# Second layer's head: the norm's and gate's four vectors loaded before the experts' summed rows

## The chip, the cores and the metric

The kernel runs on one core of a Trainium2 chip. What is measured is the device time of one execution in microseconds (us), as the median of several runs. The kernel before took 1263.39 us (three runs: 1258.64, 1263.39 and 1264.37).

## What is computed

Two layers of a generator over 256 latent tokens and 256 context tokens of 1024 numbers each. A layer normalizes and modulates its input, puts it through one projection for four kinds of attention, projects back, and ends in a mixture of 16 experts (two for each token). What matters here is the seam between the layers: the first layer's last line, and the second layer's first.

```python
for l in range(DEPTH):
    ...
    h = _layer_norm(x) * (1 + sc1) + sh1
    ...
    x = _layer_norm(ALPHA * x + g2 * _hier_moe(_layer_norm(x) * (1 + sc2) + sh2, *moe_p),
                    ln2_g[l], ln2_b[l])
    if with_ctx:
        ...
        xc = _layer_norm(ALPHA * xc + g2c * _hier_moe(_layer_norm(xc) * (1 + sc2c) + sh2c, *moe_p),
                         ln2_g[l], ln2_b[l])
```

Four vectors of 1024 numbers belong to the first layer's last line: the gate `g2` of the latent tokens, the gate `g2c` of the context tokens, and `ln2_g` and `ln2_b`. Each is spread over 128 partitions by its load, so that each load writes 128 rows of 4096 bytes.

## The kernel before

In the first layer every expert gathers its tokens' rows, runs three products, and scatters its weighted results into `yD`, a buffer in DRAM that has two rows for each token (one for each of its two experts). The very last expert's result does not go through DRAM: it stays on the core as a table `yh`, `yl` with a one-hot matrix `oh` (`combine`, L1804 and L1805), and is added by matmuls.

The second layer starts in `attention` (branch `if not full`, from L448 on). Its steps:

- **Row loads.** For each of the four chunks of 128 tokens `base` loads the two `yD` rows of each token (L1788, two loads of 512 KB for a chunk) and TensorE adds them in PSUM with an identity matrix (L1793). Chunks 0 and 1 (latent tokens) go to two `hh` tiles, chunks 2 and 3 (context) to four `s` tiles.
- **Vectors.** `fetch(vec2, vec2)` loads the four vectors by `bcast_to` (L280): key 0 (the gate of the latent tokens, in DRAM as `modD`) and `ln2_g` into one `hh` tile, `ln2_b` and key 1 (the context's gate) into another.
- **Finish.** `finish` adds the last expert (L1818, two matmuls of `kbc`/`vbc` against `qa` for each half row), multiplies by the gate (L1820), adds the residual (L1821), takes the norm (L260, ScalarE's square L262, L1826, rsqrt L222 to L232, L1831). `stream` then norms again and writes the input of the projection (L522 to L525), which TensorE turns (L507) and VectorE and ScalarE modulate (L274, L276) and split into two parts (L497, L498).
- **Weights.** `dslab` (L467) and the first slabs of the input projection (`load_slab`, L412) follow on the same queue, then small tensors: `wkvb` (L652), gains (L655), `wqb` (L657), `win_sink` (L659, 128 x 4 numbers) and the bias rows (L716). A slab is split into two parts by ScalarE (L434) and VectorE or GpSimd (L435). The attention sinks are negated by VectorE at L660.

All these loads are issued by SyncE (SP) in one queue. From `order.__enter__()` to `order.__exit__()` SP's order is the order of the code (`in_order`, a scheduler's manual mode); an SP instruction that waits for a semaphore holds back all that stand behind it. The loads take one of eight semaphores in turn, so that each load also waits for the load eight places ahead of it. VectorE and ScalarE run the lists `STEPS0` and `STEPS1` in the order of the code too, but instructions that stand outside of these lists, such as L660, are placed among them by the scheduler.

The four `hh` tiles take the places of the first layer's expert weights, one place after the other in the order in which the tiles are first written. The place that comes first was last read by the last expert's gate product (L1529), the second holds the last expert's second half of `moe_w_down` and is read until that expert's last matmul (L1548). The other two were set free earlier.

```python
            bases = [base(ch, ys[ch], sums[ch]) for ch in range(4)]
            for b in bases[:2]:
                next(b)
            fetch(vec2, vec2)
            for b in bases[2:]:
                next(b)
```

Of the kernel before, what the change touches and what calls it, by code (L numbers as in the profile page):

```python
# [91 lines left out]
def kern(tc, I, out):  # L92
# [171 lines left out]
    def in_order(*engines):  # L264

        return tc.manual_schedule(engines=set(engines))
# [81 lines left out]
    def attention(l, xs, background, mod2):  # L348
# [48 lines left out]
        def s4(shape, dt=F32):  # L397
            return P1("s4", shape, dt, bufs=9 if full else 12)
# [40 lines left out]
        def hh(shape, dt=F32R):  # L439
            return P0("hh", shape, dt, bufs=4)  # L440
# [9 lines left out]
        if not full:  # L450
            fetch, base, combine, finish = xs
            ys, b2 = ([hh([128, 2, D], F32) for _ in range(2)] for _ in range(2))
            ys = [[y[:, i] for i in range(2)] for y in ys]
            vec2 = {0: b2[0][:, 0], "ln2_g": b2[0][:, 1], "ln2_b": b2[1][:, 0], 1: b2[1][:, 1]}
            t = [s4([128, D]) for _ in range(12)]
            ys += [t[6:8], t[8:10]]
            rs = t[10:] + [r[:, :D] for r in rs]
            order = in_order(mybir.EngineType.SP)
            order.__enter__()
            sums = [[] for _ in range(4)]  # L460
            bases = [base(ch, ys[ch], sums[ch]) for ch in range(4)]
            for b in bases[:2]:
                next(b)
            fetch(vec2, vec2)
            for b in bases[2:]:
                next(b)
        SY.dma_start(dslab, wi[:, 2048:2208].rearrange("(k p) n -> p k n", p=128))  # L467
        ws.append(load_slab(slabs[0][0], (0,)))
# [1404 lines left out]
    for l in range(L):  # L1873
        mod2 = cp.tile([128, 2, 16], F32, name=f"mod2{l}")
        later = vectors((0, 1), (0, 2), (1, 0)) if l == 0 else vectors((1, 1), (1, 2))
        cur = moe(l, attention(l, cur, later, mod2), mod2)
# [28 lines left out]
```

## Time and profile before

| | us |
|---|---|
| median of three runs | 1263.39 |
| lowest and highest run | 1258.64, 1264.37 |
| the profiled execution, its own time | 1259.04 |
| its span in the trace | 1257.2 |
| TensorE busy in the span | 1104.7 (88%) |
| VectorE busy | 670.7 (53%) |
| ScalarE busy | 464.3 (37%) |
| GpSimd busy | 203.8 (16%) |

Times in the trace count from the span's start. The seam lies between about 665 and 745 us. A busy share is an average over the whole kernel; for a change of a few loads in one place, the place has to be read by itself: who waits there, for what, and which wait ends last. In the waits, `SPq` is SyncE's queue of DMA issues. An issue's row gives when SP handed the transfer over, not when the data landed; the landing shows in the start of the instruction that waited for it.

### The profile page before, as it was taken

The page shows a single profiled execution, that of the slowest core. Times are in us where ns is not written, and L with a number is a line of the kernel's source. Part 1 is how long each engine was busy: PE and PEld are TensorE (multiplying, and loading weights), DVE is VectorE, ACT ScalarE, POOL GpSimd, SP SyncE. Part 2 cuts the span into 40 slices and gives each one's busy share as a digit, 9 for nine tenths or more (in the row PEclk, how much of TensorE's full clock was granted, in tenths as well). Part 3 has the DMA queues.
Part 4 walks back from the last instruction along what each step waited for, and adds up shares of the span by engine and source line. Part 5 has one row for each costly group of instructions (what it writes and reads, how often), then busy time and mean ns, then how long its engine had stood idle before and what let it go on. Part 6 is the DMA issues. An engine that isn't in the chain of part 4 may idle for free. (4 is left out here: it accounts for less than half of the span.)

```text
span 1257.2 us, 16382 instructions
## 1 busy us (share of the span) xinstructions
PE 1104.7 (88%) x5962; PEld 701.2 (56%) x5962; DVE 670.7 (53%) x1619; ACT 464.3 (37%) x860; POOL 203.8 (16%) x222
## 2 busy tenths in 40 slices
PE   5999989899962899999898859998898799999995
PEld 2777644366851666666555347764466556455542
DVE  5377167664698785554453578637865611211113
ACT  2332165654242665444353244325643311111110
POOL 0022021212152143222211033200001200000000
PEclk9999999979975899999999979997999699999997
DMA  9943557600746799999995844534715889999993
GB/s 351 317 128 82 199 182 259 234 9 1 243 159 232 256 325 377 387 376 385 389 384 196 286 121 121 193 121 162 233 51 192 302 311 394 394 393 393 394 394 122
DMA packets 147354, 315.79 MB, mean 251 GB/s; under 512 B 20455, under 2 KB 35565, under 8 KB 142145
## 3 DMA queue, kind: packets, MB, share of 16 engines
q1 hardware_dynamic: 143284, 305.98, 68.2%
q0 software_dynamic: 3728, 8.59, 1.9%
q8 instruction: 49, 0.80, 0.3%
q14 instruction: 41, 0.33, 0.1%
q10 hardware_dynamic: 252, 0.09, 0.0%
HBM read 305.45 MB, written 13.70 MB: 254 GB/s over the span
## 5 line engine op out<-in xcount | busy, mean ns | idle before, releaser
L1439 DVE TENSOR_TENSOR hl<-rb,hl 128x1024 fp32r<-128x1024 f32 x71 | 90.7, 1302 | 58.5 <-ACT hl L1437 58.5
L1694 PE MATMUL mm<-rb,xt 128*64 128x256 f32 x816 | 101.0, 383 | 0.0
L1437 ACT ACTIVATE hl<-rb 128x1024 fp32r<-128x1024 f32 x84 | 85.8, 1054 | 34.1 <-PE mm L1449 34.0
L575 PE MATMUL mm<-s,hh 128*128 128x512 f32 x216 | 88.2, 411 | 0.0
L573 PE MATMUL mm<-s,hh 128*128 128x512 f32 x216 | 88.0, 412 | 0.0
L574 PE MATMUL mm<-s,hh 128*128 128x512 f32 x216 | 87.0, 403 | 0.0
L1694 PEld LDWEIGHTS mm<-rb,xt 128*64 128x64 f32 x816 | 58.5, 137 | 35.5 <-issue 9.0
L834 ACT ACTIVATE e<-mm,nmx 128x512 f32<-128x512 f32 (+1 forms) x96 | 58.4, 616 | 27.9 <-DVE nmx L829 17.2
L1448 PE MATMUL mm<-hl,t 128*128 128x512 f32 x144 | 61.7, 428 | 5.9 <-ACT t L1467 3.9
L1450 PE MATMUL mm<-hl,t 128*128 128x512 f32 x144 | 60.0, 419 | 6.7 <-DVE t L1468 6.7
L1449 PE MATMUL mm<-hl,t 128*128 128x512 f32 x144 | 61.7, 429 | 2.9 <-DVE hl L1439 2.7
L829 DVE TENSOR_REDUCE nmx<-mm 128x1 f32<-128x512 f32 (+1 forms) x80 | 52.5, 683 | 5.5 <-PE mm L823 4.5
L1699 DVE TENSOR_TENSOR ta<-ta,mm 128x256 f32<-128x256 f32 x16 | 6.7, 420 | 85.5 <-ACT ta L1698 85.5
L843 POOL TENSOR_SCALAR e<-e,rc 128x256 f32<-128x256 f32 x32 | 30.2, 954 | 123.1 <-DVE rc L841 111.2
L434 ACT ACTIVATE s<-ra 128x1024 fp32r<-128x1024 f32 x30 | 31.2, 1055 | 49.0 <-PE mm L575 22.4
L875 PE MATMUL tr<-cst,e 128*128 128x128 f32 x256 | 44.9, 307 | 4.0 <-DVE e L843 1.4
L573 PEld LDWEIGHTS mm<-s,hh 128*128 128x128 f32 x216 | 40.9, 190 | 13.5 <-issue 3.1
L575 PEld LDWEIGHTS mm<-s,hh 128*128 128x128 f32 x216 | 40.9, 189 | 13.2 <-issue 3.2
L574 PEld LDWEIGHTS mm<-s,hh 128*128 128x128 f32 x216 | 41.0, 190 | 12.3 <-issue 2.6
L1711 PE MATMUL mx<-rb,at 128*64 128x512 f32 x192 | 47.4, 597 | 0.0
L875 PEld LDWEIGHTS tr<-cst,e 128*128 128x128 f32 x256 | 31.9, 154 | 26.8 <-issue 14.5
L321 PE MATMUL mm<-ra,cT 128*32 128x512 f32 x320 | 43.5, 603 | 3.4 <-DMA ra<-in_w_ada_dram 3.4
(542 smaller groups left out, 2342.3 us busy)
## 6 DMA issues: line engine op xcount, KB each, us to landing
rb<-in_moe_w_up_dram SPq DMA_DIRECT2D x52, 1024.0 KB
rb<-in_moe_w_down_dram SPq DMA_DIRECT2D x50, 1024.0 KB
rb<-in_moe_w_gate_dram SPq DMA_DIRECT2D x49, 1024.0 KB
ra<-in_w_ada_dram SPq DMA_DIRECT2D x40, 1024.0 KB
ra<-in_moe_w_gate_dram SPq DMA_DIRECT2D x14, 1024.0 KB
ra<-in_w_in_dram SPq DMA_DIRECT2D x24, 512.0 KB
ra<-in_moe_w_down_dram SPq DMA_DIRECT2D x11, 1024.0 KB
ra<-in_moe_w_up_dram SPq DMA_DIRECT2D x9, 1024.0 KB
```

The lines of the kernel that those rows point to most:

```text
L573: T.matmul(ps, a, hi[:, k2], start=k == 0, stop=False)
L574: T.matmul(ps, a, lo[:, k2], start=False, stop=False)
L575: T.matmul(ps, b, hi[:, k2], start=False, stop=k == KD - 1)
L829: V.tensor_reduce(nmx[:, :nb], ps, axis=AX, op=ALU.max, negate=True)
L834: S.activation(e[:, b], ps[:, b], AF.Exp, bias=nmx[:, b:b + 1], accum_out=sm[:, b:b + 1])
L875: T.transpose(tp[:, k2, 128 * c:128 * c + 128], probs[hh][c][:, 0, 128 * kt:128 * kt + 128], ident)
L1437: S.activation(hi, w[k2], AF.Copy)
L1439: eng.tensor_tensor(lo, w[k2], hi.bitcast(F32), op=ALU.subtract)
L1448: T.matmul(ps[:C], ah, hs[:, k2], start=first and k2 == 0, stop=False)
L1449: T.matmul(ps[:C], ah, ls[:, k2], start=False, stop=False)
L1450: T.matmul(ps[:C], al, hs[:, k2], start=False, stop=last and k2 == 1)
L1694: T.matmul(ps[64 * t:64 * t + 64, j], X[:, k, gi], wt, start=k == 0, stop=k == KD - 1)
```

## The change

The four vector loads stand ahead of all eight row loads; before, they stood behind the first four of them. Nothing else is written differently, and no instruction is added or removed.

```diff
             order.__enter__()
             sums = [[] for _ in range(4)]
             bases = [base(ch, ys[ch], sums[ch]) for ch in range(4)]
-            for b in bases[:2]:
-                next(b)
             fetch(vec2, vec2)
-            for b in bases[2:]:
+            for b in bases:
                 next(b)
```

The file is two lines shorter, so that lines behind this place count two less in the changed kernel (L1788 becomes L1786, L660 becomes L658).

SP's queue at the seam, kernel before: the row loads of chunks 0 and 1, and the vectors. Names that begin with `DMAHW` are the eight semaphores of the loads, `DMASW` those of GpSimd's scatters, `PE` and `DVE` counts of those engines' work.

```order
L1788 DMA hh_6262<-yD 128x1024 [waits DMASW7_49,DMAHW5_49,DMASW0_49,PE_49]
L1788 DMA hh_6262<-yD 128x1024 [waits DMAHW6_49]
L1788 DMA hh_6263<-yD 128x1024 [waits DMAHW7_49,DMAHW4_49,PE_49]
L1788 DMA hh_6263<-yD 128x1024 [waits DMAHW0_49]
L280 DMA hh_6264<-modD_112 128x1024 [waits DMAHW1_49,DVE_49]
L280 DMA hh_6264<-in_ln_g_dram 128x1024 [waits DMAHW2_49]
L280 DMA hh_6265<-in_ln_b_dram 128x1024 [waits DMAHW3_49,DVE_49]
L280 DMA hh_6265<-modD_112 128x1024
```

The same eight loads in the changed kernel:

```order
L280 DMA hh_6264<-modD_112 128x1024 [waits DMAHW5_49,PE_49]
L280 DMA hh_6264<-in_ln_g_dram 128x1024 [waits DMAHW6_49]
L280 DMA hh_6265<-in_ln_b_dram 128x1024 [waits DMAHW7_49,DMAHW4_49,PE_49]
L280 DMA hh_6265<-modD_112 128x1024 [waits DMAHW0_49]
L1786 DMA hh_6262<-yD 128x1024 [waits DMASW7_49,DMAHW1_49,DMASW0_49,DVE_49]
L1786 DMA hh_6262<-yD 128x1024 [waits DMAHW2_49]
L1786 DMA hh_6263<-yD 128x1024 [waits DMAHW3_49,DVE_49]
L1786 DMA hh_6263<-yD 128x1024
```

The waits on the places of the tiles go with the place in the queue, not with the tile: the third load waits in both kernels for the landing and the last use of the last expert's weights (`DMAHW4`, `PE`; both kernels wait for the same counts). It was chunk 1's first row load, and is `ln2_b` now. The waits on the scatters (`DMASW`) move from the first load to the fifth.

VectorE, kernel before: the end of the second norm of chunks 0 and 1, and what follows it. `sink` is the tile of the attention sinks, `ka` and `vad` take the second parts of the first slab.

```order
L522 TENSOR_SCALAR nb_6412<-fin_1481_6324,rs_ya_6399 128x1 [waits DVE_49]
L525 TENSOR_SCALAR s_1470_6277<-x_159,fin_1481_6324,rs_ya_6399 128x1024
L660 TENSOR_SCALAR sink_6242<-sink_6242 128x4 [waits DMAHW2_49]
L435 TENSOR_TENSOR ka_6237<-ra_6293,qbc_6235 128x1024 [waits DMAHW3_49,Activation_49]
L435 TENSOR_TENSOR vad_6247<-ra_6293,vad_6247 128x1024 [waits DMASW7_49,Activation_49]
L276 TENSOR_SCALAR s_1507_6426<-tr_6430,modT_111 128x256 [waits SP_sequencer_49,Activation_49]
```

VectorE in the changed kernel, 18 instructions earlier: the end of the first norm.

```order
L260 TENSOR_SCALAR fin_1481_6324<-fin_1480_6323 128x1 [waits DVE_49]
L1829 SCALAR_TENSOR_TENSOR x_159,fin_1480_6323<-s_1470_6277,rs_yd_6349,hh_6265 128x1024
L658 TENSOR_SCALAR sink_6242<-sink_6242 128x4 [waits DMAHW2_49]
L260 TENSOR_SCALAR fin_1481_6324<-fin_1480_6323 128x1 [waits DVE_49]
L1818 TENSOR_TENSOR biasm_6244<-mm_6362,hh_6265 128x512 [waits DMAHW0_49,DMASW0_49,PE_49]
L1818 TENSOR_TENSOR biasm_6244<-mm_6365,hh_6265 128x512 [waits PE_49]
L1819 SCALAR_TENSOR_TENSOR biasm_6244,fin_1494_6382<-x_28_156,biasm_6244 128x1024 [waits DVE_49]
```

The scheduler now puts the negation of the sinks, which waits for their load, between the last two instructions of the first norm; before, it stood behind the second norm (L525). The rest of VectorE's list is the same here. Some ten instructions of TensorE, VectorE and ScalarE change places once more near the end of the second layer's attention.

## Rows read from the trace of the kernel before

**Rows 1.** Stretches by engine: busy us (instructions), granted clock, DMA share, GB/s

```profile
core 0: us, PE busy (x) PEld busy (x) DVE busy (x) ACT busy (x) POOL busy (x), PEclk, DMA share, GB/s
678.00:696.00 18.00, 15.07 (x90) 9.06 (x87) 7.63 (x9) 4.51 (x6) 3.36 (x2) 1.00 0.00 0
700.00:712.00 12.00, 9.38 (x27) 3.57 (x25) 4.20 (x8) 1.43 (x2) 0.00 (x0) 1.00 0.95 358
...
724.00:738.00 14.00, 6.35 (x25) 5.51 (x26) 8.93 (x24) 6.43 (x9) 0.00 (x0) 0.55 0.58 152
1100.00:1220.00 120.00, 117.46 (x860) 65.42 (x858) 20.23 (x42) 17.35 (x39) 0.00 (x0) 1.00 1.04 393
```

**Rows 2.** Waits of SP's DMA queue, 640 to 760 us: total, times, longest

```profile
SPq L1788 <- DMA yD<-t,idx: 29.6, 2, 23.1
...
SPq L467 <- DMA hh<-modD: 1.9, 1, 1.9
SPq L1788 <- PE mx L1548: 1.4, 1, 1.4
```

**Rows 3.** Timeline of SP at the seam: start, us, what it issues

```profile
697.85 3.41 SPq L1788 DMA_DIRECT2D hh<-yD  x4
...
700.46 0.80 SPq L1788 DMA_DIRECT2D hh<-yD  x2
...
701.37 0.36 SPq L280 DMA_DIRECT2D hh<-modD  x1
...
708.48 0.38 SPq L467 DMA_DIRECT2D ds<-in_w_in_dram  x1
...
722.28 0.71 SPq L659 DMA_DIRECT2D sink<-in_win_sink_dram  x1
```

**Rows 4.** Timeline of TensorE at the seam: start, us, what [idle before <-releaser]

```profile
676.85 1.95 PE L1529 MATMUL mm<-rb,t 128*64 128x256 f32 x16
...
701.99 0.36 PE L162 MATMUL mx<-rec 1*128 1x480 bf16 x1 [1.57 <-DVE vbc L1805]
702.28 3.70 PE L1793 MATMUL mm<-hh,cst 128*128 128x512 f32 x8
...
706.25 0.41 PE L1818 MATMUL mm<-vbc,qa 64*128 64x512 f32 x2
...
710.55 0.40 PE L1818 MATMUL mm<-vbc,qa 64*128 64x512 f32 x2
```

**Rows 5.** Timeline of VectorE at the seam

```profile
708.48 1.29 DVE L1820 TENSOR_TENSOR s<-mm,hh 128x512 f32<-128x512 f32 x2 [6.54 <-DMA hh<-in_ln_g_dram]
...
713.73 0.15 DVE L260 TENSOR_SCALAR fin<-fin 128x1 f32<-128x1 f32 x1
...
721.33 0.15 DVE L260 TENSOR_SCALAR fin<-fin 128x1 f32<-128x1 f32 x1
...
731.57 0.17 DVE L660 TENSOR_SCALAR sink<-sink 128x4 f32<-128x4 f32 x1 [4.38 <-DMA sink<-in_win_sink_dram]
731.65 1.22 DVE L435 TENSOR_TENSOR ka<-ra,qbc 128x1024 fp32r<-128x1024 f32 x1
```

**Rows 6.** Timeline of ScalarE: the first slab's first split

```profile
727.65 1.04 ACT L434 ACTIVATE qbc<-ra 128x1024 fp32r<-128x1024 f32 x1
```

**Rows 7.** The page's second part: GB/s in 40 equal slices of the span

```profile
GB/s 351 317 128 82 199 182 259 234 9 1 243 159 232 256 325 377 387 376 385 389 384 196 286 121 121 193 121 162 233 51 192 302 311 394 394 393 393 394 394 122
```

**Rows 8.** Timeline, 741 to 749 us: three small VectorE operations, and GpSimd beside them

```profile
741.62 2.28 DVE L230 TENSOR_TENSOR rs_td<-rs_td,rs_hd 128x2 f32<-128x2 f32 x1
743.93 2.27 DVE L232 SCALAR_TENSOR_TENSOR rs_yd<-rs_td,rs_yd 128x2 f32<-128x2 f32 x1
746.24 2.26 DVE L229 TENSOR_TENSOR rs_td<-rs_yd 128x2 f32<-128x2 f32 x1
748.53 0.16 DVE L230 TENSOR_TENSOR rs_td<-rs_td,rs_hd 128x2 f32<-128x2 f32 x1
...
741.48 7.00 POOL L435 TENSOR_TENSOR s<-ra,s 128x1024 fp32r<-128x1024 f32 x3 [45.91 <-ACT s L434]
```

## The prediction

> **What bounds the kernel now.** I read the stretches first, then the waits of SP's queue, then SP, TensorE and VectorE in order of time through the seam. The transfers stand still from 678 to 696 us (share 0.00) while the last large expert is computed, and run nearly full, at 358 GB/s, from 700 to 712 us [rows 1]. SP stands at the first row load, longest wait 23.1 us, until the scatters have landed [rows 2]. It issues two row loads at 697.85, and then stands again, for the last expert's last matmul: 1.4 us put down to L1548 in the waits, the next issue at 700.46 [rows 2, 3]. The vectors go out from 701.37 on [rows 3].
>
> TensorE's identity matmuls begin at 702.28, right behind L162 at 701.99, which had waited for VectorE; so chunk 0's rows were in by then. Chunk 0 is added up by 706.66 (706.25 + 0.41), chunk 1 by 710.95 [rows 4]. VectorE is idle 6.54 us until 708.48 [rows 5]. The row names the transfer of `ln2_g`, but SP's next load, which waits for `modD`, goes out at the same 708.48 [rows 2, 3]; what ended the wait was the gate's vector. So VectorE has 1.82 us (708.48 - 706.66) in which it waits for the vector alone. This is what the change can take away at this place.
>
> The seam has a second wait. VectorE stands 4.38 us at L660 until 731.57 for the attention sinks, a load of 2 KB issued at 722.28 behind everything else in the queue [rows 3, 5]. The first split of the weights (L435), which heads the list that leads to the projection, follows it at 731.65 [rows 5]. Behind the seam no slack shows that could take it up: the last experts keep TensorE busy 117.46 of 120 us [rows 1], so I take what the seam loses or wins as it is to the end.
>
> **The change, part by part.**
>
> *Two of four vectors leave the path.* `modD` and `ln2_g` wait for the place that L1529 reads until 678.80 (676.85 + 1.95) [rows 4]. They go out then, into transfers at rest [rows 1], and cost nothing; without that rest they would cost two transfers. VectorE's wait for the gate's vector goes, at most 1.82 us. What is late next is chunk 0 itself.
>
> *The other two come in front of the rows.* `ln2_b` is now the third load, and waits for L1548 as the third load did before: 700.46. All eight row loads stand behind it. The first one takes the place in the queue that `modD` had, fifth, and goes out at about 701.4 instead of 697.85 [rows 3]. When does it land? The nearest rows: from an empty queue, issue to use was at most 4.43 us (697.85 to 702.28); as fifth of a full queue, 7.11 us (701.37 to 708.48) [rows 3 to 5]. The row load is now third behind 700.46, so it lands between 705.8 and 708.5. I take 707.0, between the two. TensorE then starts 4.7 us later than 702.28, and chunk 1 leaves VectorE (L260, 713.73) at 718.4.
>
> *The sinks' wait moves forward.* The negation now stands in front of the L260 that ran at 721.33 [rows 5]. VectorE gets there at about 726.0 (721.33 + 4.7) and waits for the sinks there. Behind it, all of VectorE's 18 instructions from that L260 to L525 stand still, and with them ScalarE, whose L434 at 727.65 follows L524 in its list [rows 6].
>
> *When do the sinks land?* From 700.46 on the queue carries ten loads of 512 KB ahead of the small ones, where it carried twelve from 697.85: the start is 2.61 us later, and two loads are gone. A load is 0.524 MB; at 358 GB/s [rows 1] it takes 1.46 us, and the sinks come 2.61 - 2 x 1.46 = -0.31 us, that is 0.3 us earlier, at 731.26. Bounds: at the fastest slice, 394 GB/s [rows 7], a load takes 1.33 us and they come at 731.52; by the five transfers up to the landing of `modD`, (708.48 - 697.85) / 5 = 2.13 us [rows 3], at 729.92. I take 358 GB/s, which is of this very stretch. The Trainium skill, "DMA: Bandwidth & Descriptors", section "Specifications", gives 435 GB/s as the fabric's ceiling; by it a load would take an estimated 1.21 us, the sinks would come 0.19 us later, and the sum below would be 0.5 us higher. The trace has no slice that fast.
>
> *The sum.* With the sinks at 731.26, L260 starts 0.08 us later (as L435 did behind L660 [rows 5]), at 731.34, which is 10.01 us later than before. ScalarE's first split ends at 728.69 + 10.01 = 738.70 (727.65 + 1.04 [rows 6]), and L435, which needs it, starts there instead of at 731.65: **7.05 us later**. The 4.7 us by which the rows are late vanish in this wait, and the 1.82 us gained do too; they are not added. By the bounds of the sinks' landing the loss is 5.7 to 7.3 us. The instructions that change places near the end of the attention I cost at nothing: they are the same operations, and TensorE has other work beside them.
>
> On the profiled execution this makes 1259.04 + 7.05 = 1266.1 us. That execution and the lowest run (1258.64) lie near 1259, the other two near 1264, and the median, 1263.39, is one of the upper pair. I count from the mean of the four, 1261.36, which gives **1268.4 us**.
>
> **The rivals.**
>
> *The rows alone.* If the 2 KB of sinks land before VectorE needs them, the sinks cost nothing at all. This decides at 726.0: before that, only the 4.7 us count, ScalarE's split ends at 733.39, and L435 is 1.74 us late, or 0.5 us if the rows land at 705.8: at most 1263.1 us. For it: the sinks are small. Against it: they are issued last, and took 9.3 us from 722.28.
>
> *GpSimd's collisions fall elsewhere: not slower.* Three operations of VectorE take 2.28, 2.27 and 2.26 us beside GpSimd's splits, where an undisturbed one takes 0.16 [rows 8]. If GpSimd's first split starts so much earlier or later against VectorE's list that they no longer meet, 6.81 - 3 x 0.16 = 6.33 us come back of the 7.05, and the time is 1262.1. It decides at a shift of some 2.3 us, one such operation. Against it: both engines wait for the same ScalarE splits, so both should shift together. The Trainium skill, "SBUF — State Buffer", section "SBUF: two separate sides", says that the port pair of VectorE and GpSimd is an exclusive lock, held for a whole instruction; by that rule the three do come back when they no longer meet, and the 2.3 us against GpSimd's 7.00 for three agree.
>
> *TensorE's clock falls.* TensorE now has no work from the last expert's end to 707.0. In the stretch from 724 on, which follows a pause, the granted clock is a mean of 0.55 of 2.4 GHz, so mostly 1.2 GHz, while from 700 to 712 it is 1.00 [rows 1]. If chunks 0 and 1 ran at 1.2 GHz throughout, their 8.67 us (702.28 to 710.95 [rows 4]) would double, VectorE would reach the sinks' wait at 734.7, after their landing, and L435 would be 10.4 us late: 1271.8. Up to 5 us of such loss stay hidden in the wait (726.0 to 731.3). The Trainium skill, "TensorE: Matmul & The Clock Gate", section "Part 1: The HAM clock gate (the "warmup" mystery)", has the idle array fall to 1.2 GHz and return only after sustained work; the row from 724 us agrees, and by that rule part of this loss comes, though hardly all.
>
> *The change does what its order says.* If no load waited for L1548, all four vectors would be out of the way, chunk 1 would still leave TensorE at 710.95, and the sinks, four loads earlier, would end VectorE's wait near 725.7: still about 1.5 us late. The order of SP shows that two loads do wait, so I give this no chance of its own.
>
> **How the numbers follow.** The forecast gets 0.60; its own range, bounds and spread of the runs (2.9 us to either side of their mean) together, is 1264.2 to 1271.6. The rows alone get 0.14, the collisions 0.08, the clock 0.13; 0.05 is left for the reordering at the attention's end winning or losing several us. A measurement of this kernel can tell about 0.5% from no change, 6.3 us: from 1257.1 to 1269.7 is the same. The forecast lies across that border: a little over half of it (0.33) is slower, the rest (0.27) the same. The clock is mostly slower (0.10), the first two rivals are the same (0.22). This gives slower 0.44, same 0.52, faster 0.04. The range, 1262 to 1273, takes in most of the two smaller rivals and the clock's.
>
> **What would show it.** Right: `modD` and `ln2_g` issued near 679 us, `ln2_b` at the last expert's end, the first row load about 0.9 us behind it; TensorE's identity matmuls (L1791 there) starting at 706 to 708.5; VectorE's idle time before L658 about 5 us, ending near 731; L435 near 738.7. Wrong: sinks that land before 727, identity matmuls that start before 704, or later stretches that are shorter than before by several us.

## The result and the profile after

The changed kernel took 1268.59 us (median of 14 runs), the kernel before 1262.34 us beside it. The ratio, estimated from the fast runs alone (one of the 14 ran in a slower state), is 1.0055 with an interval of 1.0038 to 1.0072; the medians by themselves give 1.0050. So it is slower, and the size lies on the border of the half per cent up to which the prediction called a time the same. The profiled execution has a span of 1263.7 us against 1257.2. The work is the same. By the page's first part TensorE's busy time grew by 2.7 us, VectorE's and GpSimd's by 0.4 at most, ScalarE's not at all:

```profile
span 1263.7 us, 16383 instructions
...
PE 1107.4 (88%) x5962; PEld 701.3 (55%) x5962; DVE 670.9 (53%) x1619; ACT 464.3 (37%) x860; POOL 204.2 (16%) x222
```

The queue first, as the timeline of SP at the seam; it answers to [rows 3].

```profile
678.48 0.34 SPq L280 DMA_DIRECT2D hh<-modD  x1
678.87 0.43 SPq L280 DMA_DIRECT2D hh<-in_ln_g_dram  x1
700.14 0.33 SPq L280 DMA_DIRECT2D hh<-in_ln_b_dram  x1
...
701.12 2.22 SPq L1786 DMA_DIRECT2D hh<-yD  x4
...
721.27 0.96 SPq L657 DMA_DIRECT2D sink<-in_win_sink_dram  x1
```

Its longest wait between 640 and 760 us, against [rows 2]:

```profile
SPq L280 <- PE mx L1546: 20.7, 1, 20.7
```

Two vectors go out at 678.5, in the quiet. The third waits 20.7 us for the last expert's last matmul, and the first row load stands behind it until 701.12; before it went out at 697.85. Counted from the start of `vbc`, VectorE's last operation for the last expert (701.19 before, 700.86 now), that is 3.60 us later. TensorE's timeline shows what that costs (against [rows 4]):

```profile
701.67 0.36 PE L162 MATMUL mx<-rec 1*128 1x480 bf16 x1 [1.57 <-DVE vbc L1803]
707.43 5.69 PE L1791 MATMUL mm<-hh,cst 128*128 128x512 f32 x8 [5.41 <-DMA hh<-yD]
...
713.72 3.70 PE L1791 MATMUL mm<-hh,cst 128*128 128x512 f32 x8
```

TensorE stands 5.41 us for the rows. Then chunk 0's eight identity matmuls take 5.69 us, where chunk 1's, and chunk 0's before, take 3.70. The stretches of the changed kernel show why (columns as in [rows 1]): the granted clock begins to fall while TensorE stands, is 0.50 of 2.4 GHz, that is 1.2 GHz, when chunk 0 is added, and comes back to 1.00 only between 710 and 712 us.

```profile
704.00:705.00 1.00, 0.00 (x0) 0.00 (x0) 0.00 (x0) 0.00 (x0) 0.00 (x0) 0.82 1.06 397
...
708.00:710.00 2.00, 2.00 (x3) 0.68 (x2) 0.00 (x0) 0.00 (x0) 0.00 (x0) 0.50 1.00 404
710.00:712.00 2.00, 2.00 (x4) 0.87 (x3) 0.00 (x0) 0.00 (x0) 0.00 (x0) 0.63 1.04 424
712.00:714.00 2.00, 2.00 (x8) 0.77 (x7) 0.18 (x1) 0.00 (x0) 0.00 (x0) 1.00 1.02 414
```

VectorE's timeline, which answers to [rows 5]:

```profile
713.82 1.29 DVE L1818 TENSOR_TENSOR s<-mm,hh 128x512 f32<-128x512 f32 x2 [12.21 <-PE mm L1816]
...
730.17 0.17 DVE L658 TENSOR_SCALAR sink<-sink 128x4 f32<-128x4 f32 x1 [1.88 <-DMA sink<-in_win_sink_dram]
...
737.59 1.23 DVE L435 TENSOR_TENSOR ka<-ra,qbc 128x1024 fp32r<-128x1024 f32 x1 [1.53 <-ACT qbc L434]
```

It no longer waits for the gate's vector but for TensorE, and starts at 713.82 instead of 708.48. It reaches the negation of the sinks at 728.29 (730.17 - 1.88), stands there 1.88 us, and L435 starts at 737.59 instead of 731.65: 5.94 us late. From L435 to the end of the span it is 526.11 us, before 525.55. So the seam holds 5.94 of the 6.5 us by which the span is longer.

### The profile page after: what moved, and what is told of

Its sections match the earlier page's. It is cut to its first block, busy times and chain, and to the rows that moved or that the text cites. A ratio compares the mean times of both kernels' runs of the same rounds, so it can differ in the third digit from the quotient of the medians.

```text
span 1263.7 us, 16383 instructions
## 1 busy us (share of the span) xinstructions
PE 1107.4 (88%) x5962; PEld 701.3 (55%) x5962; DVE 670.9 (53%) x1619; ACT 464.3 (37%) x860; POOL 204.2 (16%) x222
```

## The experiments

Executions reach the seam up to 9 us apart, so single profiles are compared by a distance: from the start of `vbc` to the start of L435. It is 737.59 - 700.86 = 36.73 us in the changed kernel and 731.65 - 701.19 = 30.46 in the kernel before (VectorE's timeline, the changed kernel first):

```profile
700.86 0.75 DVE L1803 SCALAR_TENSOR_TENSOR vbc<-mx,tw,kbc 128x512 fp32r<-128x512 f32 x1 [4.60 <-ACT kbc L1802]
...
701.19 0.75 DVE L1805 SCALAR_TENSOR_TENSOR vbc<-mx,tw,kbc 128x512 fp32r<-128x512 f32 x1 [4.60 <-ACT kbc L1804]
```

The table's distances come from such rows. The two theories: the sinks' wait ends last and hides most of the late rows (the prediction), or the late rows themselves are most of the loss. All runs together (the first identity matmul is counted from `vbc` too; "sinks" says how long VectorE stands before the negation; ratios are to the kernel before):

| run | first identity matmul | chunk 0's eight | sinks | L435 | ratio, interval |
|---|---|---|---|---|---|
| before | 1.09 | 3.70 | 4.38 | 30.46 | |
| after | 6.57 | 5.69 | 1.88 | 36.73 | 1.0055 (1.0038 to 1.0072) |
| 1 after, sinks on GpSimd | 6.49 | 6.34 | none | 35.41 | 1.0042 (1.0021 to 1.0063) |
| 2 before, sinks on GpSimd | 1.09 | 3.70 | none | 27.36 | 0.9982 (0.9960 to 1.0003) |
| 3 before, negation early | 1.09 | 3.70 | 10.07 | 37.59 | 1.0087 (1.0064 to 1.0111) |
| 4 rows not held, sinks on GpSimd | 1.09 | 3.70 | none | 27.38 | 0.9966 (0.9947 to 0.9985) |
| 5 after, 28 matmuls added | 6.90 | 3.70 | 0.75 | 33.98 | 1.0033 (1.0008 to 1.0058) |
| 6 run 1, 28 matmuls added | 6.89 | 3.70 | none | 33.17 | 1.0039 (1.0009 to 1.0069) |
| 7 rows not held | 1.10 | 3.70 | 5.55 | 32.97 | 1.0038 (1.0009 to 1.0068) |
| 8 two vectors ahead, sinks on GpSimd | 2.91 | 5.40 | none | 30.90 | 1.0011 (0.9983 to 1.0039) |
| 9 after, 25 matmuls added | 6.66 | 3.70 | 4.13 | 37.07 | 1.0049 (1.0027 to 1.0071) |
| 10 after, sinks loaded first | 6.62 | 5.73 | none | 34.94 | 1.0027 (1.0004 to 1.0050) |
| 11 rows not held, sinks loaded first | 3.73 | 5.40 | none | 31.71 | 0.9999 (0.9977 to 1.0021) |
| 12 the same, behind two vectors | 1.09 | 3.78 | none | 27.46 | 0.9963 (0.9934 to 0.9993) |

### Runs 1 and 2: the sinks taken from VectorE

```diff
-        V.tensor_scalar(sink[:, 1], sink[:, 0], -1.0, None, op0=ALU.mult)
+        (V if full else G).tensor_scalar(sink[:, 1], sink[:, 0], -1.0, None, op0=ALU.mult)
```

Run 1 is the changed kernel with this edit, run 2 the kernel before. Expected of run 1:

> Changed kernel, with the negation of the second layer's sinks on GpSimd instead of VectorE; all else in the same order. It takes the wait for the sinks out of VectorE's list and leaves the late rows. By the prediction's step (rows 4.7 us late, mostly hidden by the sinks) L435 starts 1.7 us later than in the kernel before, near 733.4, and the time is +1.7 us on the kernel before (ratio 1.001). By the trace of the changed kernel (rows late by 7 us, the sinks only 1.9 us of the loss) L435 starts near 735.7, +4.0 us on the kernel before (1.003). If the sinks did not matter at all, it stays at 737.6, +6 us.

Expected of run 2:

> Kernel before, with the same negation on GpSimd. If the sinks' wait at L660 is on the path in the kernel before too, L435 starts when ScalarE's first split ends, at 728.7 instead of 731.65, and the time is 3.0 us shorter (ratio 0.998). If the wait is hidden there, nothing changes (1.000).

Run 1, by the timeline of TensorE and VectorE:

```profile
708.30 0.75 DVE L1803 SCALAR_TENSOR_TENSOR vbc<-mx,tw,kbc 128x512 fp32r<-128x512 f32 x1 [4.60 <-ACT kbc L1802]
714.79 6.34 PE L1791 MATMUL mm<-hh,cst 128*128 128x512 f32 x8 [5.32 <-DMA hh<-yD]
...
743.71 1.23 DVE L435 TENSOR_TENSOR ka<-ra,qbc 128x1024 fp32r<-128x1024 f32 x1 [1.53 <-ACT qbc L434]
```

It shows 35.41, 4.95 us behind the kernel before; its chunk 0 took 0.65 us longer than in the changed kernel. So the late rows, with the slower clock behind them, cost 4 to 5 us against the kernel before, not the 1.7 us that the prediction gave the rows. Run 2 comes out at 27.36: in the kernel before the sinks' wait cost 3.10 us (30.46 - 27.36), as worked out. The distance shows this; the time of run 2 alone (interval 0.9960 to 1.0003) does not. VectorE waits for ScalarE alone there, as its timeline in run 2 shows:

```profile
707.15 0.75 DVE L1805 SCALAR_TENSOR_TENSOR vbc<-mx,tw,kbc 128x512 fp32r<-128x512 f32 x1 [4.60 <-ACT kbc L1804]
...
734.51 1.23 DVE L435 TENSOR_TENSOR ka<-ra,qbc 128x1024 fp32r<-128x1024 f32 x1 [1.53 <-ACT qbc L434]
```

### Run 3: only the negation moved

The loads keep the order of the kernel before. The small loads are written ahead of the list `STEPS0`, and the negation has a step of its own (91) in it:

```diff
-STEPS0 = (90, -1, 90, -2, 0, 0, 0, 0, -3, 0, 0, -4, 1, 0, 2, 3, 0, 1, 4, 5, 0, 1)
+STEPS0 = (90, -1, 90, -2, 0, 0, 0, 0, -3, 0, 0, 91, -4, 1, 0, 2, 3, 0, 1, 4, 5, 0, 1)
```

> Kernel before, loads in its own order, with only the negation moved to the place in VectorE's list that it has in the changed kernel (one instruction later, behind the L260). If a wait for the sinks there is enough to lose the time, VectorE stands about 10 us there until 731.6, L435 starts near 738.9, and the time is +7.3 us (ratio 1.006), with rows that are not late at all. If the late rows are what costs, L435 stays near 731.7 and the time at 1.000. Some instructions behind the seam change places with this edit; L435 is read first.

VectorE's timeline:

```profile
702.44 0.75 DVE L1812 SCALAR_TENSOR_TENSOR vbc<-mx,tw,kbc 128x512 fp32r<-128x512 f32 x1 [4.60 <-ACT kbc L1811]
...
732.63 0.17 DVE L569 TENSOR_SCALAR sink<-sink 128x4 f32<-128x4 f32 x1 [10.07 <-DMA sink<-in_win_sink_dram]
...
740.03 1.23 DVE L435 TENSOR_TENSOR ka<-ra,qbc 128x1024 fp32r<-128x1024 f32 x1 [1.53 <-ACT qbc L434]
```

A wait of 10.07 us for 2 KB, and L435 7.13 us late, with no row late at all. The place of this one instruction is enough to lose, at L435, what the whole change loses. The time lost (ratio 1.0087) is more than the 7.1 us; in the profile some 3 us more lie behind the seam (528.97 us from L435 to the end), where this edit also changes the order. That part was not followed up, and runs 1 and 9 have as much there (528.49 and 529.23).

### Runs 4 and 7: the rows not held

`ln2_b` and the context's gate go through GpSimd's queue; their tile keeps the place that is free only after the last expert.

```diff
-        SY.dma_start(b, bass.AP(tensor=row_ap.tensor, offset=row_ap.offset, ap=[[0, 128], [1, D]]))
+        (q or SY).dma_start(b, bass.AP(tensor=row_ap.tensor, offset=row_ap.offset, ap=[[0, 128], [1, D]]))
...
-            fetch(vec2, vec2)
+            fetch(vec2, (0, "ln2_g")), fetch(vec2, ("ln2_b", 1), G)
```

Run 4 also has the sinks on GpSimd:

> Changed kernel, but ln2_b and the context's gate go through GpSimd's queue (they keep the place that is free only after the last expert), and the sinks are negated on GpSimd as in the first run. If the third load's wait for the last expert is what makes the rows late, the first row load goes out at 697.9 again, the identity matmuls start near 702.3, L435 near 728.7, and the time is 3 us below the kernel before (0.998), as in the second run. If the rows are late for another reason (the transfers, two queues at once), L435 stays near 735.7 as in the first run, +4 us.

Run 7 leaves them on VectorE:

> Changed kernel with ln2_b and the context's gate through GpSimd's queue, as in the fourth run, but the sinks negated on VectorE; the scheduler puts that behind the two L1818 of chunk 2. The rows are early again; only the wait for the sinks is left. If it ends last, VectorE gets to it about 20.6 us after L162 and stands until the sinks land, at 26 to 28.5, and L435 starts at 32 to 34.5, later than in the kernel before (29.66) by 2.5 to 5 us. If the rows were the whole loss, L435 starts at 26.6 as in the fourth run.

The timeline of run 4, SP, TensorE and VectorE:

```profile
701.90 1.75 SPq L1786 DMA_DIRECT2D hh<-yD  x4
705.25 0.75 DVE L1803 SCALAR_TENSOR_TENSOR vbc<-mx,tw,kbc 128x512 fp32r<-128x512 f32 x1 [4.60 <-ACT kbc L1802]
706.34 3.70 PE L1791 MATMUL mm<-hh,cst 128*128 128x512 f32 x8
...
710.74 1.29 DVE L1818 TENSOR_TENSOR s<-mm,hh 128x512 f32<-128x512 f32 x2 [4.74 <-PE mm L1816]
...
715.04 1.29 DVE L1818 TENSOR_TENSOR s<-mm,hh 128x512 f32<-128x512 f32 x2 [1.55 <-PE mm L1816]
...
732.63 1.23 DVE L435 TENSOR_TENSOR ka<-ra,qbc 128x1024 fp32r<-128x1024 f32 x1 [1.53 <-ACT qbc L434]
```

With the third load out of SP's queue the rows are on time: in run 4 the first identity matmul starts 1.09 us after `vbc`, as before, and at full clock. L435 stands at 27.38, and the ratio to the kernel before is 0.9966, with an interval that leaves out 1. But run 2, with the vectors in their old place, has L435 at 27.36. With the sinks out of the way, the early vectors gain nothing at L435: VectorE begins with chunk 0 earlier (5.49 us after `vbc`, before 7.29) and then stands 1.55 us for the sum of chunk 1.

In run 7 VectorE, whose negation the scheduler places a little differently here, stands for the sinks until 26.93 us after `vbc`:

```profile
727.93 0.17 DVE L658 TENSOR_SCALAR sink<-sink 128x4 f32<-128x4 f32 x1 [5.55 <-DMA sink<-in_win_sink_dram]
```

L435 stands at 32.97. With rows on time the sinks' wait alone puts it 5.59 us behind run 4 and 2.51 us behind the kernel before.

### Runs 5, 6 and 9: TensorE kept busy in the pause

```diff
                 ps = mm([128, 512])
+                for _ in range(28 if ch + t == 0 else 0):
+                    T.matmul(ps, last[2][0:64, 0:128], last[0][0:64, :512], start=True, stop=True)
                 for i in range(2):
```

> Changed kernel, with 28 more matmuls (the last expert's table against its one-hot matrix, overwritten by chunk 0's first identity matmul) while TensorE waits for the rows; all that is added is work that nobody reads. Times count from the start of L162. In the changed kernel chunk 0's eight identity matmuls took 5.69 us and L435 starts at 35.9. If the pause lowers TensorE's clock, they now take about 3.7 us. If the sinks' wait ends last, as the prediction has it, VectorE only stands 2 us longer at the negation (3.9 instead of 1.9) and L435 stays at 35.9; the time is that of the changed kernel, +6 us on the kernel before (1.005). If the late rows and the clock end last, L435 comes 2 us earlier, at 33.9.

> The first run (sinks negated on GpSimd) with the same 28 matmuls. There L435 started 34.6 us after L162, and chunk 0's identity matmuls took 6.34 us. If the clock is 2.6 us of that loss, they take 3.7 us and L435 starts at about 32.0, +2.3 us on the kernel before (29.66). If the pause is not what slows them, both stay (34.6).

L162 itself fell behind the added matmuls in both, so they are read from `vbc` (0.81 us ahead of L162 in the changed kernel). Run 5 decides nothing: the scheduler put the negation four instructions later, where VectorE had other work and waited 0.75 us. Run 6 gives the clock's price: chunk 0 takes 3.70 us instead of 6.34, and L435 comes 2.24 us earlier than in run 1, although the added matmuls made the start 0.4 us later. Run 9 repeats run 5 with 25 matmuls, which leaves VectorE's order alone:

> The fifth run once more with 25 added matmuls instead of 28, so that the negation keeps the place on VectorE that it has in the changed kernel (with 28 the scheduler put it four instructions later). Times count from the start of VectorE's last operation for the last expert (vbc, L1803), which the added work can't move; there L435 stands at 36.73 in the changed kernel, and VectorE's idle time before the negation is 1.88 us. Chunk 0's eight identity matmuls should take 3.7 us again instead of 5.69. If the sinks end last, as the prediction has it, VectorE stands 1.9 + 2.0 = 3.9 us before the negation and L435 stays at 36.7. If the rows end last, L435 comes 2 us earlier, at 34.7.

The timeline of TensorE and VectorE in run 9:

```profile
703.62 5.96 PE L1791 MATMUL mm<-kbc,qa 64*128 64x512 f32 x25 [0.79 <-ACT kbc L1804]
...
710.26 3.70 PE L1793 MATMUL mm<-hh,cst 128*128 128x512 f32 x8 [0.38 <-DMA hh<-yD]
...
733.25 0.17 DVE L658 TENSOR_SCALAR sink<-sink 128x4 f32<-128x4 f32 x1 [4.13 <-DMA sink<-in_win_sink_dram]
...
740.67 1.23 DVE L435 TENSOR_TENSOR ka<-ra,qbc 128x1024 fp32r<-128x1024 f32 x1 [1.53 <-ACT qbc L434]
```

VectorE arrives 2 us earlier and stands 2.25 us longer (4.13 against 1.88); L435 stays (37.07; the sinks came 0.34 us later in this execution). So in the changed kernel the sinks do end last. What the rows lose in front of them up to that point costs nothing.

### Runs 8, 10, 11 and 12: which place in the queue

Run 8 moves two vectors only (and has the sinks on GpSimd):

```diff
+            fetch(vec2, (0, "ln2_g"))
             for b in bases[:2]:
                 next(b)
-            fetch(vec2, vec2)
+            fetch(vec2, ("ln2_b", 1))
```

> Only the two vectors go ahead whose place is free early (the latent gate and ln2_g); ln2_b and the context's gate stand behind the rows of chunks 0 and 1, as in the kernel before. The place that the last expert holds now falls to chunk 0's rows. Sinks on GpSimd. If the price of the change is that held place, the first row load goes out 1.5 us before L162 (700.14 in the changed kernel) instead of 4.1, the identity matmuls start 2.9 to 4.7 us after L162, and L435 at 29.2 to 31.7: 3 to 5 us earlier than with all four ahead (34.6), but later than in the second run (26.6), where chunk 1 met that place. If only the count of loads ahead mattered, L435 would be at 26.6.

The held place now falls to chunk 0's rows. They go out 1.5 us before L162 and are used 2.10 us behind its start, earlier than the 2.9 to 4.7 that were expected; but chunk 0 takes 5.40 us, which the expectation left out. So L435, at 30.90 (30.09 from L162), is within what was expected by two errors against each other. It is 3.5 us behind run 2. Runs 10 to 12 load the sinks early and leave GpSimd's arithmetic alone: run 10 the changed kernel, run 11 the kernel of run 7, both with the sinks' load ahead of the vectors; run 12 with it behind the first two vectors.

```diff
+            g = I["win_sink"][l]
+            SY.dma_start(sink[:, 0], bass.AP(tensor=g.tensor, offset=g.offset, ap=[[0, 128], [1, 4]]))
             sums = [[] for _ in range(4)]
             bases = [base(ch, ys[ch], sums[ch]) for ch in range(4)]
...
-        SY.dma_start(sink[:, 0], bass.AP(tensor=g.tensor, offset=g.offset, ap=[[0, 128], [1, 4]]))
+        if full:
+            g = I["win_sink"][l]
+            SY.dma_start(sink[:, 0], bass.AP(tensor=g.tensor, offset=g.offset, ap=[[0, 128], [1, 4]]))
```

> Changed kernel with the second layer's sinks loaded first of all, ahead of the vectors, and negated on VectorE right behind vbc; no GpSimd. The late rows stay. If only the landing of the sinks mattered in the first run, and not the engine, L435 stands where the late rows put it: 34.8 us after vbc where chunk 0 takes 5.7 us, 35.4 where it takes 6.3; the kernel before has 30.46, so the time is +4.3 to +5 us on it (1.004). If GpSimd itself gave something, it stays near 36.7.

Run 10 confirms run 1: 34.94. The sinks' load does not go out early here either (703.13, 6.19 us before `vbc`), and the two vectors stand behind it; since the rows stand behind `ln2_b` in any case, they are no later for it (6.62 against 6.57).

> Both cures without an operation on GpSimd: sinks loaded first, and ln2_b and the context's gate through GpSimd's queue so that no row load waits for the last expert. If the two waits are the whole account, L435 starts 27.4 us after vbc, 3.1 us earlier than in the kernel before, and the time is 0.997 of it, as in the fourth run. If the fourth run gained by something else, the ratio is 1.000 or more.

Run 11 missed: 31.71 instead of 27.4. SP's longest wait in it, and the timeline of SP and TensorE:

```profile
SPq L461 <- PE mm L1530: 26.7, 1, 26.7
...
694.05 0.35 SPq L461 DMA_DIRECT2D sink<-in_win_sink_dram  x1
694.45 0.43 SPq L280 DMA_DIRECT2D hh<-modD  x1
...
697.73 2.79 SPq L1789 DMA_DIRECT2D hh<-yD  x4
...
703.97 5.40 PE L1794 MATMUL mm<-hh,cst 128*128 128x512 f32 x8 [2.57 <-DMA hh<-yD]
```

The sinks' own place was not free before 694.05 (the wait is for L1530, the last of the gate products), so the load of 2 KB held the two vectors behind it for some 16 us (694.45 against 678.48 in the changed kernel), and their 1 MB then stood in front of the rows. It is the error of the change once more, made in the experiment.

> The eleventh run with the sinks' load one step further back: behind the latent gate and ln2_g, still ahead of the rows. In the eleventh run the sinks' place came free only at 694.05, so the two vectors behind that load went out 15 us later than in the changed kernel, their transfers met the rows', and L435 stood at 31.7 instead of 27.4 us after vbc. If that is why it missed, the vectors go out near 679 again, the identity matmuls start 1.1 us after vbc and take 3.7 us, and L435 stands at 27.4: 3.1 us less than in the kernel before, a ratio of about 0.997. If GpSimd's loads or the early sinks slow the rows by themselves, L435 stays near 31.7 and the ratio at 1.000.

The same timeline of run 12, with VectorE's L435:

```profile
685.34 0.35 SPq L280 DMA_DIRECT2D hh<-modD  x1
...
701.50 0.33 SPq L464 DMA_DIRECT2D sink<-in_win_sink_dram  x1
704.78 1.94 SPq L1789 DMA_DIRECT2D hh<-yD  x4
...
708.78 3.78 PE L1794 MATMUL mm<-hh,cst 128*128 128x512 f32 x8
...
735.15 1.23 DVE L435 TENSOR_TENSOR ka<-ra,qbc 128x1024 fp32r<-128x1024 f32 x1 [1.53 <-ACT qbc L434]
```

One step further back the vectors leave in the quiet again, and L435 stands at 27.46. The ratio is 0.9963, with run 4's the lowest; run 2, at 27.36 and 0.9982, cannot be told from them.

**The account.** Where no sinks are waited for, L435 stands at 27.36 (run 2), plus what the first identity matmul is later than 1.09, plus what chunk 0 takes over 3.70. For run 1 that is 27.36 + 5.40 + 2.64 = 35.40 (measured 35.41), for run 6 33.16 (33.17), for run 8 30.88 (30.90), for run 10 34.92 (34.94), for run 11 31.70 (31.71). The changed kernel would be at 27.36 + 5.48 + 1.99 = 34.83; its sinks end 1.90 us later, at 36.73. The kernel before has 3.10 us of sinks in it. So the change's 6.27 us are 5.48 of late rows, 1.99 of clock and 1.90 of sinks, less the 3.10 that the sinks cost anyway. Of the 5.48, SP's later issue is 3.60; the other 1.88 lie between the issue of the rows and their use.

## Why the prediction was right, and where not

- **The queue: right.** Two vectors at 678.5, `ln2_b` at the last expert's end (700.14), the rows behind it (701.12; forecast 701.4). Runs 4 and 7 show that this hold is what makes the rows late. The Trainium skill, "DMA: Bandwidth & Descriptors", section "Anatomy of one DMA — SWDGE (gpsimd) path", which is about loads that GpSimd issues, says that the semaphore wait of a DMA is done by the issuing sequencer before dispatch; SP's 20.7 us in front of L280, with the free row loads behind it, show the same in SP's queue.
- **What the change can take away: wrong.** The prediction put it at VectorE's 1.82 us of waiting for the vector alone. But in the kernel before VectorE takes up chunk 1 at 711.14, 0.19 us after its sum is done (710.95). So all but some 0.2 us of the 1.82 could only turn into a wait for chunk 1, as in run 4 (27.38 against 27.36 of run 2). The sum did not suffer, since it let the 1.82 us vanish. VectorE's row in the kernel before:

```profile
711.14 1.28 DVE L1820 TENSOR_TENSOR s<-mm,hh 128x512 f32<-128x512 f32 x2
```

- **The rows' landing: right.** 707.43 against 707.0, inside the bounds of 705.8 and 708.5.
- **The clock: the step that failed.** The sum ran chunk 0 at full clock, and full loss at 1.2 GHz was a rival with 0.13. The truth lay between: 1.99 us, all of it in chunk 0. So VectorE came to the negation at 728.29, not 726.0, and stood 1.88 us, not 5. The Trainium skill, "TensorE: Matmul & The Clock Gate", section "Part 1: The HAM clock gate (the "warmup" mystery)", has the clock fall when the array idles and return after sustained work; the granted clock of 0.82 in the pause (704 to 705 us), 0.50 from 708 to 710 and 1.00 from 712 agrees, and run 9, without the pause, has 3.70 us.
- **The sinks' landing: the mis-sized term.** Forecast 731.26, measured 730.17. The last expert ended 0.32 us earlier in this execution. The rest is the load: from the first held load to the sinks it took 33.72 us with twelve large loads (697.85 to 731.57 [rows 3, 5]) and 30.03 with ten (700.14 to 730.17), so a load is worth 1.85 us by this pair of executions, where 1.46 was taken; the bounds, 1.33 and 2.13, held it. Runs 3 and 9, with the same two orders of loads, give 1.58 (33.54 and 30.38), so part of the error is the spread between executions. The earlier landing moves the sum from 7.05 to the 5.94 us read at L435.
- **"The 4.7 us ... vanish in this wait": right in the end, by a small margin.** Run 9 shows that 2 us fewer in front of the sinks change nothing. But the rows were 7.5 us late (5.48 + 1.99), and the wait covered them with 1.9 us to spare. That is why the sum survived the failed step: it hung on the sinks' landing alone.
- **The rival "the rows alone": its price was wrong.** 1.74 us was worked out; runs 1 and 10 give 4.95 and 4.48 (35.41 and 34.94, less 30.46), mostly since the clock was missing in it (2.64 and 2.03 us); the rest is that the rows were later than 4.7 us (5.40 and 5.53).
- **GpSimd's collisions: did not fall elsewhere.** The three small operations beside L435 are there again, 6 us later like everything else (timeline of VectorE and GpSimd, against [rows 8]):

```profile
747.56 2.27 DVE L230 TENSOR_TENSOR rs_td<-rs_td,rs_hd 128x2 f32<-128x2 f32 x1
749.87 2.28 DVE L232 SCALAR_TENSOR_TENSOR rs_yd<-rs_td,rs_yd 128x2 f32<-128x2 f32 x1
752.18 2.26 DVE L229 TENSOR_TENSOR rs_td<-rs_yd 128x2 f32<-128x2 f32 x1
...
747.42 7.01 POOL L435 TENSOR_TENSOR s<-ra,s 128x1024 fp32r<-128x1024 f32 x3 [52.18 <-ACT s L434]
```

- **Behind the seam: right, as far as it can be seen.** 526.11 us against 525.55. The profiles of the other runs have 524.05 (run 12) to 529.23 (run 9) there, so a price of a us or two for the reordering at the attention's end can't be ruled out.

The median, 1268.59, lies 0.2 us from the forecast of 1268.4. That closeness is partly luck: the loss at L435 was 1.1 us smaller than the sum, and the kernel before, at 1262.34 beside it, 1.0 us above the 1261.36 that the sum was counted from.

## What to carry to other kernels

A load that is written earlier is not issued earlier if its place in memory is still in use; in a queue with a fixed order it then holds everything behind it, so look up for each load when its destination comes free, and put the held one behind what is needed sooner, or in another queue (runs 4 and 12). Before an instruction that waits is moved, by hand or by a scheduler, look at who stands behind it: here the negation of 2 KB cost 3.10 us in its old place, 10.23 in the new one (run 3 against run 2) and nothing on GpSimd. Before a wait is taken away, look at what its engine would wait for next: behind the 1.82 us for the vector stood chunk 1's sum, so the change had almost nothing to win. And where a wait ahead of TensorE grows by some microseconds, count the slower clock after it as well.

## What the hardware showed that was not expected

A short pause already brought the lower clock. In the changed kernel, where TensorE stood 5.41 us, the clock fell within the pause (0.82 from 704 to 705 us). In run 8 TensorE stood 1.57 us, ran one matmul of 0.36 and stood 1.75 us more; chunk 0 then took 5.40 us instead of 3.70. There the clock was still 1.00 in the pause and fell only when TensorE was busy again (stretches of run 8, columns as in [rows 1]):

```profile
705.00:707.00 2.00, 0.30 (x1) 0.30 (x2) 0.00 (x0) 0.00 (x0) 0.00 (x0) 1.00 0.97 369
707.00:709.00 2.00, 2.00 (x5) 0.71 (x4) 0.00 (x0) 0.00 (x0) 0.00 (x0) 0.76 0.91 326
709.00:711.00 2.00, 2.00 (x4) 0.96 (x3) 0.00 (x0) 0.00 (x0) 0.00 (x0) 0.50 1.04 315
711.00:713.00 2.00, 2.00 (x7) 0.64 (x7) 0.20 (x1) 0.00 (x0) 0.00 (x0) 0.89 0.96 281
```

In the kernel before and in run 4, where only the first 1.57 us stand there, chunk 0 runs at 3.70.
